# Six pairs of gate projections per layer as seven products of quarters, in a stage of their own

## The chip, the cores and the metric

The kernel runs on one core of one Trainium2 chip. The metric is the device time of one execution in microseconds (us). Before the change the median of three runs is 2574.22 us (2568.73 to 2576.42).

TensorE (PE in the profile) multiplies, ScalarE (ACT), VectorE (DVE) and GpSimd (POOL) do the elementwise work, and SyncE (SP) issues all of this kernel's DMAs from one in-order queue. Each engine carries out its own instructions in the order in which they stand in the built program and waits on semaphores for what the others deliver.

## The reference

Two layers of a decoder trunk over 1024 tokens behind 16 learned meta tokens (L = 1040 columns), width 1024. In each layer one wide projection of the normed input feeds three attention branches and their gates:

```python
h = rmsnorm(x, norm_g)
proj = h @ w_in
(a_q, a_k, a_v, a_f, a_z, b_cq, b_ckv, b_kr, b_z,
 c_q, c_k, c_v, c_z, gates) = jnp.split(proj, np.cumsum(SPLIT_SIZES)[:-1], axis=-1)
y_a = causal_block_attention(..., log_cum)                   # A: 8 heads, forget bias
y_b = causal_block_attention(q_b, k_b, v_b, ...)             # B: latent, 8 heads
y_c = sliding_window_sink_attention(qc, kc, vc, sinks)       # C: banded, window 128
branches = jnp.stack([y_a * silu(a_z), y_b * silu(b_z), y_c * silu(c_z)], axis=2)
proj_br = jnp.einsum('blnw,nwd->blnd', branches, w_branch)
g = jax.nn.sigmoid(gates.reshape(B, L, N_BRANCH, D_MODEL))
return x + jnp.sum(g * proj_br, axis=2) @ w_out
```

`gates` is a product of the 1040 normed tokens (1024 in the second layer, where meta tokens are no longer needed as queries) with 3072 columns of `w_in`: 24 tiles of 128 output channels per layer. Only these are changed.

## The kernel before, in words

Activations lie transposed, channels on the 128 partitions and tokens along the free dimension. Every float32 value that enters a large product is split in two rounded parts, a high and a low one (`split`: ACT writes the high part, DVE or POOL subtracts it from the source for the low part), and `mm3` makes each product of three matmuls: high by high, low activations by high weights, high activations by low weights. The normed input is `hh` and `hl`, eight tiles of 128 channels by 1040 tokens each.

A projection tile (`proj`) is 8 x 3 matmuls for each chunk of tokens: chunks of 264, 264 and 512 columns in the first layer (`FULL`), 512 and 512 in the second (`TOK`). `weights` loads one 512 KB weight tile (`wr`, two buffers), casts it on ACT to `wh` and subtracts on POOL for `wl`.

The stages of a layer, in program order: values of branch A and C (`values`), banded projections (`wq`: rotary keys and queries of branch C; the small rows of the forget gate run beside them in `side_work`), low-rank projections (`lr`, `vb`, `mq`), then forgetting attention (tiles `ks`, `qq`, `ql`), banded attention (`kc`, `cqq`, `cql`, `sP`), latent attention (`kt`, `qt`), the merge of the branches and the output projection. The merge reads the gates back from DRAM (`gate_d`) and applies the sigmoid as a tanh.

The 24 gate tiles, and twelve gate tiles of another kind (`z`, for the SiLU), need nothing but `hh` and `hl`. Before, all 24 are made by `gate`, at places given by two tables. `EARLY` puts two (first layer) or one (second) into the low-rank stage. `PLAN` has one list for each attention stage; each call of `fill` takes the next entry and writes one projection for each letter (`g` a gate, `z` a SiLU gate, `r` and `s` parts of the merge). So these projections fill TensorE while softmax work is under way.

What is written this way is not the final order. The tile framework schedules all instructions of the program against its own timeline when the kernel is built, so matmuls of a gate end up between matmuls of attention, and instructions move over tens of microseconds. The built order is fixed from then on.

Banded attention works in steps of 128 queries for four heads: eight matmuls of 256 columns (`qk`: high and low queries by keys), a reduction on DVE for each head, exponentials on ACT, eight transposes, a split by ACT and DVE, and four matmuls of 512 columns. There are sixteen steps in a layer, eight for each of the two key heads, and one short step for the meta tokens in the first layer. Its loads reuse memory of the forgetting attention and stand behind `rt_d` in SP's queue, which carries the reciprocal row sums (`rcp`) of the last heads there.

## Time and profile before

| | before |
|---|---|
| median of three runs | 2574.22 us |
| profiled execution | 2569.85 us, its span 2567.8 us |
| TensorE busy | 2517.1 us, 98% of the span, 15446 matmuls |
| VectorE, ScalarE, GpSimd busy | 1273.4, 1205.8, 1012.9 us (50%, 47%, 39%) |
| granted TensorE clock, mean | 0.998 |
| DMA queue, share of 16 engines | 38.0% |

A matmul's row shows its whole way through the array, so rows overlap: 350 ns is the mean of a 512-column matmul whose successor starts some 232 ns later. Time per matmul is therefore read from start to start, and a wait shows somewhat too short as idle time.

The stages of the profiled execution, by the rows of the timeline: first layer values to about 85 us, banded projections to 150, low-rank stages to 300, forgetting attention to 645, banded attention to 815, latent attention to 1085, merge and output projection to 1290. The second layer's forgetting attention ends at 1920, its banded attention at 2080, its latent attention at 2360.

### The profile page before, as it was taken

The numbers are of one execution on the slowest core, as the hardware profiler recorded it, in microseconds if no ns is written. First come the engines' busy times: TensorE is split into PE (matmuls) and PEld (weight loads), VectorE is DVE, ScalarE is ACT, GpSimd is POOL, SyncE is SP. The second block draws the span as 40 slices with busy tenths as digits, with TensorE's granted clock in tenths as the row PEclk, the third lists the DMA queues.
The fourth block names the chain that finished last, engine by engine and source line by source line (L and its number), as shares of the span: only waits on it lengthen the run. The fifth ranks groups of instructions, "written<-read, shape, count | busy, mean of one in ns | idle before, by whom it ended". The sixth has DMA issues, their size and how long they took to land.

```text
span 2567.8 us, 42092 instructions
## 1 busy us (share of the span) xinstructions
PE 2517.1 (98%) x15446; PEld 2247.5 (88%) x15446; DVE 1273.4 (50%) x3279; ACT 1205.8 (47%) x2704; POOL 1012.9 (39%) x990
## 2 busy tenths in 40 slices
PE   8999999999999999999999999999999999999998
PEld 7999899999888999899998888888887888887797
DVE  6454355544363445657156463545434623565643
ACT  5234355545374556654233343555435634566433
POOL 2241545443332424463523325454423342353644
PEclk9999999999999999999999999999999999999999
DMA  5244512222634434364333353221326362453532
GB/s 170 62 136 150 189 54 82 73 78 77 172 105 115 129 101 126 102 228 166 114 90 99 97 198 138 66 88 56 98 69 176 100 169 81 124 146 115 183 130 74
DMA packets 137630, 303.39 MB, mean 118 GB/s; under 512 B 22560, under 2 KB 63296, under 8 KB 137424
## 3 DMA queue, kind: packets, MB, share of 16 engines
q1 hardware_dynamic: 137424, 300.71, 38.0%
q8 instruction: 122, 2.00, 0.3%
q14 instruction: 84, 0.69, 0.1%
HBM read 211.98 MB, written 88.66 MB: 117 GB/s over the span
## 4 chain that ended last, share of the span: by engine, by line
PE 79%; DMA 5%; DVE 2%; ACT 2%; POOL 2%; issue 1%; SPq 0%; POOLq 0%; ACTq 0%; DVEq 0%
PE ps_pj L175 14%; PE ps_pj L176 14%; PE ps_pj L177 14%; PE ps_t L268 5%; PE ps_s L1001 3%; PE ps_o L312 3%; PE ps_o L310 2%; PE ps_s L177 2%; PE ps_s L176 2%; PE ps_s L175 2%; PE ps_s L804 1%; PE ps_s L802 1%; PE ps_o L176 1%; PE ps_o L177 1%; PE ps_o L175 1%
## 5 line engine op out<-in xcount | busy, mean ns | idle before, releaser
L158 POOL TENSOR_TENSOR wl<-wr,wh 128x1024 fp32r<-128x1024 f32 (+1 forms) x156 | 376.1, 2411 | 776.7 <-ACT wh L157 653.5
L175 PE MATMUL ps_pj<-hh,wh 128*128 128x512 f32 (+1 forms) x1920 | 672.7, 350 | 3.5 <-ACT gt L657 2.0
L176 PE MATMUL ps_pj<-hl,wh 128*128 128x512 f32 (+1 forms) x1920 | 671.0, 349 | 0.0
L177 PE MATMUL ps_pj<-hh,wl 128*128 128x512 f32 (+1 forms) x1920 | 669.6, 349 | 0.9 <-POOL wl L158 0.9
L175 PEld LDWEIGHTS ps_pj<-hh,wh 128*128 128x128 f32 x1920 | 361.3, 188 | 46.7 <-ACT gt L657 2.6
L177 PEld LDWEIGHTS ps_pj<-hh,wl 128*128 128x128 f32 x1920 | 361.5, 188 | 42.3 <-POOL wl L158 1.1
L176 PEld LDWEIGHTS ps_pj<-hl,wh 128*128 128x128 f32 x1920 | 361.4, 188 | 39.4 <-issue 0.5
L158 DVE TENSOR_TENSOR ptl<-ps_t,pth 128x512 fp32r<-128x512 f32 (+1 forms) x386 | 244.5, 640 | 143.6 <-ACT pth L157 137.8
L260 ACT ACTIVATE P<-P,mn 128x656 f32<-128x656 f32 (+8 forms) x272 | 207.0, 761 | 165.1 <-DVE mn L255 160.5
L157 ACT CAST pth<-ps_t 128x512 fp32r<-128x512 f32 (+1 forms) x386 | 205.7, 546 | 165.3 <-PE ps_t L268 131.9
L157 ACT CAST wh<-wr 128x1024 fp32r<-128x1024 f32 (+1 forms) x156 | 162.1, 1039 | 237.0 <-PE ps_pj L176 134.5
L268 PE MATMUL ps_t<-ident,P 128*128 128x128 f32 x1152 | 186.2, 275 | 0.8 <-DVE ptl L158 0.7
L310 PE MATMUL ps_o<-pth,vp 128*128 128x256 f32 (+1 forms) x640 | 167.2, 277 | 2.7 <-DVE u L281 1.7
L312 PE MATMUL ps_o<-ptl,vp 128*128 128x256 f32 (+1 forms) x640 | 159.4, 287 | 2.7 <-DVE ptl L158 2.5
L298 POOL COPY pmeta<-P 128x16 f32<-128x16 f32 x256 | 49.3, 196 | 270.1 <-ACT P L260 261.9
L1001 PE MATMUL ps_s<-kt,qt 96*128 96x328 f32 (+9 forms) x696 | 146.4, 327 | 2.7 <-DVE mn L255 2.6
L268 PEld LDWEIGHTS ps_t<-ident,P 128*128 128x128 f32 x1152 | 134.2, 140 | 8.6 <-DVE ptl L158 1.5
L310 PEld LDWEIGHTS ps_o<-pth,vp 128*128 128x128 f32 x640 | 120.6, 189 | 11.2 <-ACT pth L157 1.7
L809 POOL TENSOR_TENSOR cm<-ckb,tri 128x128 f32<-128x128 f32 (+1 forms) x136 | 60.3, 445 | 175.2 <-DVE mn L255 171.4
L312 PEld LDWEIGHTS ps_o<-ptl,vp 128*128 128x128 f32 x640 | 120.6, 188 | 9.6 <-DVE ptl L158 5.6
L281 DVE TENSOR_TENSOR u<-ps_o,hv 64x256 f32<-64x256 f32 x128 | 53.9, 421 | 135.4 <-ACT hv L280 120.2
L1001 PEld LDWEIGHTS ps_s<-kt,qt 96*128 96x128 f32 (+1 forms) x696 | 108.0, 186 | 10.1 <-DVE mn L255 5.2
(354 smaller groups left out, 5641.7 us busy)
## 6 DMA issues: line engine op xcount, KB each, us to landing
wr<-in_w_dram SPq DMA_DIRECT2D x108, 512.0 KB
gate_d<-gt SPq DMA_DIRECT2D x72, 256.0 KB
gt<-gate_d SPq DMA_DIRECT2D x24, 520.0 KB
wr<-in_wbr_dram SPq DMA_DIRECT2D x24, 512.0 KB
gt<-gate_d SPq DMA_DIRECT2D x24, 512.0 KB
kn_d<-sg SPq DMA_DIRECT2D x16, 520.0 KB
ckb<-ck_d SPq DMA_DIRECT2D x16, 520.0 KB
kt<-kn_d SPq DMA_DIRECT2D x16, 520.0 KB
```

The source lines that it names most:

```text
L157: nc.scalar.copy(hi, src)
L158: (eng or nc.vector).tensor_tensor(lo, src, _f(hi), ALU.subtract)
L175: nc.tensor.matmul(dst, w1, rh[:, k, c0:c1], start=(k == 0), stop=False)
L176: nc.tensor.matmul(dst, w1, rl[:, k, c0:c1], start=False, stop=False)
L177: nc.tensor.matmul(dst, wl[:, k * P:k * P + m], rh[:, k, c0:c1], start=False, stop=(k == nk - 1))
L260: nc.scalar.activation(s[:rows, :n], s[:rows, :n], AF.Exp, bias=prev, scale=-1.0, accum_out=total)
L268: nc.tensor.transpose(t[:kk, c:c + rows], src, ident[:rows, :rows])
L281: nc.vector.tensor_tensor(u[mine, :n], o[mine, :n], t[mine, :n], ALU.add)
L310: nc.tensor.matmul(dst, vp[:, j + x, vs], ph[:, cols], start=(j + x == 0), stop=False)
L312: nc.tensor.matmul(dst, vp[:, j + x, vs], pl[:, cols], start=False, stop=(diag and x == 1))
L809: nc.gpsimd.tensor_tensor(cm[:rows, :rows], ckb[:rows, d:n], tri[:rows, :rows], ALU.add)
L1001: nc.tensor.matmul(dst, q[:, qi, q0:q0 + rows], kt[:, ki, c0:c1], start=(x == 0), stop=(x == 2))
```

## The change

In each layer the first twelve gate tiles of the list are taken two at a time (`SEVEN = (6, 6)`). A pair is a product of a weight matrix of 256 output channels by 1024 inputs with `h`, 1024 inputs by 1040 (1024) tokens. Both are cut in quarters, halves of the channels and of the inputs by halves of the tokens (`KH = 4` channel tiles, `HW` = 520 or 512 tokens). Eight quarter products become seven, with sums of quarters formed before and after (Strassen's scheme in Winograd's form).

```diff
+        def hidden_sums():
+            for k in range(KH):
+                d = difference(k, (0, 1), (0, 0))        # 3 tensor_tensor on DVE
+                done(0, k, d)                            # split: ACT cast, DVE subtract
+                for i, b_ in ((1, (1, 1)), (3, (1, 0))):
+                    n = tt_.tile([P, HW[0]], F32, tag="tt2", name="tt", bufs=2)[:, :hw]
+                    tensor(n, _f(hidden(0, *b_)[:, k]), d, sub)
+                    tensor(n, n, _f(hidden(1, *b_)[:, k]), add)
+                    done(i, k, n)
+                    d = n
+                yield
+                done(2, k, difference(k, (1, 1), (0, 1)))
+                yield
...
-        values(va, 0, ws, KD, hh, hl, rest, span=1 if first else 2)
+        values(va, 0, ws, KD, hh, hl, rest, between=sums_at, span=1 if first else 2)
...
+        def gate_pairs(n):
+            gs = tc.alloc_tile_pool(name=f"gs{l}", bufs=2, side=B if first else A, reuse_waits="tile")
+            chunks = [(0, hw // 2), (hw // 2, hw)] if first else [(0, hw)]
...
+                split(a1h, a1l, raws[0], eng=nc.gpsimd)
...
+                for f, x, y, op in ((f1, r21, r22, ALU.add), (f2, f1, r11, ALU.subtract),
+                                    (f3, r11, r21, ALU.subtract), (f4, r12, f2, ALU.subtract)):
+                    nc.gpsimd.tensor_tensor(f, x, y, op)
+                for j in (1, 0, 2, 3):
+                    split(s[j][0], s[j][1], fs[j], eng=nc.gpsimd)
+                split(*a22, r22, eng=nc.gpsimd)
...
+                product(a11, b11, (x1, None))
+                product(s[1], t2, (x2, x1))
+                product(a12, b21, (x4, x1))
+                store(0, 0, x4)
+                product(s[0], t1, (x1, x2))
+                product(s[2], t3, (x3, x1), (x2, x2))
+                store(1, 1, x3)
+                product(s[3], b22, (x1, x1))
+                store(0, 1, x1)
+                product(a22, t4, (x2, x2))
+                store(1, 0, x2)
+        gate_pairs(SEVEN[l])
```

Each `product` is 4 x 3 matmuls for a chunk, of 260 columns (two chunks, first layer) or 512 (second); its result leaves PSUM by an ACT copy or by DVE additions. `gate_pairs` stands between the banded projections and the low-rank stage, and both layers have one. The hidden sums (`ths`, eight tiles) are written into the values stage from its fifth (third) block on. The other edits make room: the small rows of `side_work` share tiles, the pairs of rotated rows in the banded projections have two buffers instead of three, `krt` and `ths` have pools of their own, and `vw` is released earlier.

The tables lose the twelve gates. In all there were 9, 7 and 6 gates in the three lists of the first layer and 9, 9 and 5 in the second (forgetting, banded, latent); now there are 3, 4, 3 and 4, 4, 3. The list of the second layer's banded stage shows it:

```diff
-     "gg zg z g . gg zz g gg".split(),
+     "g zg z . . g zz . g".split(),
```

The first place to look at is where the second layer's banded attention begins, on PE: `rcp` is the transpose of the last row sums of the forgetting stage, `pmeta` and `pm,vm` finish its meta keys, `hh,wh`, `hl,wh` and `hh,wl` are projections of the filler, and `kc,cqq` is banded attention. Before:

```order
L312 MATMUL ps_o<-ptl,vp 128x128
L331 MATMUL ps_t<-ident,rcp 16x128
L364 MATMUL ps_t<-ident,pmeta 32x128 x4
L176 MATMUL ps_pj<-hl,wh 128x512
L177 MATMUL ps_pj<-hh,wl 128x512
L175 MATMUL ps_pj<-hh,wh 128x512
```

After:

```order
L336 MATMUL ps_t<-ident,rcp 16x128
L315 MATMUL ps_o<-pth,vp 128x256
L317 MATMUL ps_o<-ptl,vp 128x256
L315 MATMUL ps_o<-pth,vp 128x128
L317 MATMUL ps_o<-ptl,vp 128x128
L369 MATMUL ps_t<-ident,pmeta 32x128 x8
L376 MATMUL ps_o<-pm,vm 128x512 x2
L988 MATMUL ps_s<-kc,cqq 128x256
L990 MATMUL ps_s<-kc,cql 128x256
```

Before, 57 filler matmuls stand between `rcp` and the first `kc,cqq`, and more between the next seven; now there is none, and the whole first step of banded attention (eight such matmuls) and the first two transposes of its exponentials come before the next filler. In the first layer it is the same: 87 filler matmuls of 512 or 264 columns stood between `rcp` and the first `kc,cqq`, and 39 more between that and the eighth; now none.

SP's queue at this place after the change, 16 DMAs in nine rows; the loads of banded attention stand behind `rt_d`, which waits for `rcp`:

```order
L106 DMA rt_d<-rt 8x128 x2
L106 DMA sw<-in_swm_dram 128x512
L106 DMA rb<-rt_d 64x1024 x2
L106 DMA vcr<-vc_d 128x1024
L106 DMA vcr<-vc_d 16x128
L106 DMA kc<-sk_d 128x16
L106 DMA kc<-sk_d 128x1024
L106 DMA cqq<-sq_d 64x1024 x2
L106 DMA cql<-sq_d 64x1024
```

This order is the one of before; in the first layer four stores of gates (`gate_d<-gt`) that stood among the loads are gone. Three more groups of `cqq`, `cql` follow for the other heads.

The third place is the middle of the second layer's banded attention on PE, where the steps of the first key head end (`rcp`) and those of the second begin. Before:

```order
L892 MATMUL ps_o<-pth,vc 128x512
L331 MATMUL ps_t<-ident,rcp 32x128
L867 MATMUL ps_s<-kc,cqq 128x256
L869 MATMUL ps_s<-kc,cql 128x256
L177 MATMUL ps_pj<-hh,wl 128x512
L867 MATMUL ps_s<-kc,cqq 128x256
L869 MATMUL ps_s<-kc,cql 128x256
```

After:

```order
L1015 MATMUL ps_o<-ptl,vc 128x512
L336 MATMUL ps_t<-ident,rcp 32x128
L1013 MATMUL ps_o<-pth,vc 128x512
L988 MATMUL ps_s<-kc,cqq 128x256
L990 MATMUL ps_s<-kc,cql 128x256
L988 MATMUL ps_s<-kc,cqq 128x256
L990 MATMUL ps_s<-kc,cql 128x256
L273 MATMUL ps_t<-ident,sP 128x128 x4
```

The filler matmuls between the steps are gone here: from the sixth step to the fifteenth no filler stands in PE's queue (80 `kc` matmuls, 72 transposes and 31 matmuls of 512 columns in one piece), and then a whole gate tile stands in one block of 48. In the first layer such a piece has 45 `kc` matmuls, 36 transposes and 14 products with `vc`, which is about half as long. In latent attention the pieces without filler that hold over 4.2 us of matmuls add up to 142 us by the durations in the profile before, against 78 us; in forgetting attention to 46 us against 6.

## The prediction

> **What bounds the kernel now.** I read the page first, then the pace of TensorE from the timeline, then the places where it waits.

> ```profile
> span 2567.8 us, 42092 instructions
> PE 2517.1 (98%) x15446; PEld 2247.5 (88%) x15446; DVE 1273.4 (50%) x3279; ACT 1205.8 (47%) x2704; POOL 1012.9 (39%) x990
> PE   8999999999999999999999999999999999999998
> PEclk9999999999999999999999999999999999999999
> ```

> TensorE is the bound nearly everywhere, at full clock, while the others work half the time. So a matmul less is time gained, but only while something keeps TensorE's queue fed. Rows of matmuls overlap, so the price of one is read from start to start, here in second and first layer:

> ```profile
> 1921.16 0.39 PE L177 MATMUL ps_pj<-hh,wl 128*128 128x512 f32 x1
> ...
> 1925.11 0.40 PE L176 MATMUL ps_pj<-hl,wh 128*128 128x512 f32 x1
> ```

> ```profile
> 646.40 0.29 PE L175 MATMUL ps_pj<-hh,wh 128*128 128x264 f32 x1
> ...
> 649.19 0.28 PE L177 MATMUL ps_pj<-hh,wl 128*128 128x264 f32 x1
> ```

> The first pair is 17 matmuls apart, so 3.95 / 17 = 0.232 us for 512 columns; the second 23, so 2.79 / 23 = 0.121 us for 264. By the line through both, 260 columns take 0.1195.

> **Removed: an eighth of the products.** In the first layer a pair took 96 x 0.121 + 48 x 0.232 = 22.8 us and will take 7 x 12 x 2 = 168 x 0.1195 = 20.1; in the second 96 x 0.232 = 22.3 becomes 84 x 0.232 = 19.5. Over six pairs each that is 6 x (2.7 + 2.8) = 33 us. [...]

> **Added, and hidden.** The sums of hidden quarters are 4 x 14 = 56 DVE operations and 16 ACT casts per layer. DVE's nearest row with two SBUF operands takes 0.69 us, so some 39 us per layer, in the values stage:

> ```profile
> L958 DVE TENSOR_TENSOR acc<-acc,gt x80: 420/691/4335, 1116.9 to 2463.8; 128x512 f32<-128x512 f32 x48, 128x264 f32<-128x264 f32 x32
> ```

> ```profile
> 60.00:80.00 20.00, 20.00 (x130) 19.65 (x129) 1.56 (x4) 1.54 (x8) 0.00 (x0) 1.00 0.14 42
> 80.00:100.00 20.00, 20.00 (x134) 18.77 (x133) 2.85 (x7) 2.84 (x13) 0.00 (x0) 1.00 0.12 36
> 1340.00:1360.00 20.00, 20.00 (x130) 19.82 (x129) 2.29 (x6) 1.88 (x11) 0.00 (x0) 1.00 0.14 42
> ```

> In these windows (PE, PEld, DVE, ACT, POOL busy) DVE is idle for 35.6 of 40 us, so the sums cost 0; what spills into the banded projections could cost up to 3. Without that cover the 39 us would delay the rotations there.

> In the new stage POOL makes per pair one difference of 1024 columns and nine operations of 512:

> ```profile
> L158 POOL TENSOR_TENSOR wl<-wr,wh 128x1024 fp32r<-128x1024 f32 (+1 forms) x156 | 376.1, 2411 | 776.7 <-ACT wh L157 653.5
> ```

> ```profile
> 133.32 1.30 POOL L158 TENSOR_TENSOR wvl<-wr,wvh 128x512 fp32r<-128x512 f32 x1 [0.72 <-ACT wvh L157]
> ```

> 2.4 + 9 x 1.3 = 14.1 us against 20 of TensorE: hidden, with 6 us left for loading the next weights. At the entry it is not: in the built order POOL starts the sums behind the last rotation of the banded projections, and the first product with a sum needs four operations (5.2 us) on top of the rotation's POOL and DVE work (about 4). In the first layer TensorE has 48 matmuls (5.7 us) for this, so 4 us wait; in the second another product stands ahead and 1 us is left. Together +5, between 0 and 10. The stores of the results and weight loads share SP's queue; nobody behind them is short. The pools with two buffers instead of three wait for stores while TensorE has four chunks in PSUM: 0.

> **Moved: cover taken from attention.** Twelve gates per layer, some 137 us of ready work, leave the queue between attention's matmuls. The largest effect is at the entry of banded attention. In the second layer:

> ```profile
> 1920.38 0.27 PE L331 MATMUL ps_t<-ident,rcp 128*16 128x128 f32 x1
> ...
> 1935.07 0.28 PE L867 MATMUL ps_s<-kc,cqq 128*128 128x256 f32 x1
> 1937.71 0.36 PE L867 MATMUL ps_s<-kc,cqq 128*128 128x256 f32 x1 [0.39 <-DMA cqq<-sq_d]
> 1941.06 0.35 PE L867 MATMUL ps_s<-kc,cqq 128*128 128x256 f32 x1 [0.39 <-DMA cqq<-sq_d]
> ...
> 1944.96 0.28 PE L869 MATMUL ps_s<-kc,cql 128*128 128x256 f32 x1
> ```

> ```profile
> 1921.26 0.62 SPq L101 DMA_DIRECT2D rt_d<-rt  x2
> ...
> 1936.43 0.44 SPq L101 DMA_DIRECT2D cql<-sq_d  x1
> ```

> ```profile
> 1924.00:1927.00 3.00, 3.00 (x17) 2.39 (x16) 0.41 (x1) 1.16 (x2) 2.89 (x5) 1.00 1.01 229
> 1942.00:1945.00 3.00, 2.78 (x13) 1.97 (x13) 0.00 (x0) 0.00 (x0) 0.00 (x0) 1.00 1.04 328
> ```

> The loads stand behind `rt_d`, which waits for `rcp`, and with a DMA share of 1.0 they last until the fourth head's matmul runs at 1944.96, 24.6 us after `rcp`. Fillers cover that now, up to some 3 us. In the built order after the change they are gone: PE has four `vp` matmuls, eight transposes, two `pm` matmuls (1.9 us) and the step itself (1), and then must wait about 21. Net +18: at least +14, if the loads run at the best rate of these windows; at most +21 with the first transposes' wait for the exponentials. Everything behind it on PE is held. The first layer:

> ```profile
> 644.65 0.27 PE L331 MATMUL ps_t<-ident,rcp 128*18 128x128 f32 x1
> ...
> 668.57 0.18 PE L869 MATMUL ps_s<-kc,cql 128*16 128x16 f32 x1 [0.24 <-DMA cql<-sq_d]
> ```

> 23.9 us, less 3.5 for four gate stores (0.8 MB at some 230 GB/s) that are no longer among the loads, less 2.5 of own matmuls, less 3 that is waited there already: +14, between 10 and 18.

> A wait of that length also costs clock:

> ```profile
> 12.96 0.64 PE L454 MATMUL ps_pj<-wvh,hh 128*128 128x320 f32 x1 [3.21 <-ACT hh L157]
> ```

> ```profile
> 10.00:15.00 5.00, 1.95 (x6) 1.52 (x7) 3.10 (x11) 4.78 (x13) 5.00 (x4) 0.79 1.09 342
> 15.00:20.00 5.00, 5.00 (x34) 5.00 (x34) 2.88 (x11) 3.07 (x13) 5.00 (x4) 0.87 1.06 379
> ```

> After 3.2 us of idle TensorE two windows show a clock of 0.79 and 0.87, 5 x (0.21 + 0.13) = 1.7 us lost. Two waits: +3, between 2 and 6.

> Next, the steps of banded attention without filler:

> ```profile
> L873 DVE CUSTOM_DVE_ANT_0 sP<-ps_s,sw,nsink 128x256 f32<-128x256 f32 x64 | 28.3, 477 | 23.3 <-PE ps_s L869 23.3
> L158 DVE TENSOR_TENSOR ptl<-ps_t,pth 128x512 fp32r<-128x512 f32 x32 | 21.6, 683 | 0.6 <-ACT pth L157 0.2
> L902 DVE TENSOR_TENSOR u<-ps_o,stt 64x128 f32<-64x128 f32 x64 | 15.6, 283 | 24.8 <-ACT stt L900 23.3 <-DMA y_d<-u 1.1
> ```

> These are sixteen steps, so (28.3 + 21.6 + 15.6) / 16 = 4.1 us of DVE per step, while PE's share is 8 x 0.12 + 8 x 0.11 + 4 x 0.232 = 2.8. With a filler DVE is hidden; without, a step takes at least 4.1. DVE is not busy all the time even where little fills, as the latent stage shows:

> ```profile
> 900.00:920.00 20.00, 20.00 (x140) 18.72 (x138) 8.94 (x25) 9.31 (x21) 2.97 (x4) 1.00 0.29 81
> 1020.00:1040.00 20.00, 19.30 (x140) 17.83 (x140) 16.12 (x50) 16.19 (x41) 15.16 (x23) 1.00 0.70 183
> 1040.00:1060.00 20.00, 18.50 (x135) 16.88 (x134) 15.87 (x45) 15.66 (x38) 17.83 (x23) 1.00 0.20 75
> 2240.00:2260.00 20.00, 18.13 (x129) 15.79 (x128) 15.81 (x47) 16.55 (x39) 16.60 (x18) 1.00 0.77 200
> ```

> There it is busy for 0.8 of the time, so a step would take 5.1. I take 4.6, the middle. The second layer's piece without filler is about nine steps by its 80 `kc` matmuls, 72 transposes and 31 products: 9 x 4.6 = 41 us against 25 of PE, less about 1 that DVE still works off behind the next block of 48: +15, between 10 and 21. The first layer's, four and a half steps: 20.7 less 12.3 less 1: +7, between 3 and 10.

> Latent attention without filler: the covered window 900:920 shows no idle time, the three bare ones 0.7 to 1.9 of 20, and the gaps behind modelled ends hide about as much again. So 0.05 to 0.25 us per us of such PE work, 0.15 in the middle; the pieces grow from 78 to 142 us: +10, between 3 and 16. Forgetting attention's pieces are short (5 to 9 us) and DVE lags little: +2, between 0 and 8.

> **The sum**: -33 + 5 + 18 + 14 + 3 + 15 + 7 + 10 + 2 = +41 us on the profiled execution's 2569.85. That execution lies 4.4 below the median of the runs; +41 on the median 2574.22 is 2615.

> **Rivals.**
> 1. Cover survives: faster. The place is the entry of banded attention. If TensorE found its loads landed, both waits and their clock (35) would go; if steps also ran at PE's 2.8 us (22 more), -33 + 5 + 12 = -16 remains, 2558. It decides once the loads take under some 10 us after `rcp`. For it: two entries only, and loads could be better packed. Against: the share of 1.0 says that the data itself takes that time. Chance 0.07.
> 2. The entries wait, but the bare steps run near PE's pace, since work lags and is made up in the next block: 22 less, and half of latent attention's 10: 2588. For it: single steps without filler are short. Against: nine in a row. Chance 0.18.
> 3. The clock falls in the bare pieces too. Scattered idle time there is 7 to 9% in the windows above, at a clock of 1.00, which speaks against it; if steps of 2.8 us PE in 4.6 drop it to half, the 37 us of banded pieces and parts of the next blocks lose about 20 us: 2635. [...] Chance 0.10.
> 4. The change does not make its product cheaper: POOL's 14.1 us and a weight load in series exceed 20 us per pair, TensorE waits for sums. At 23 us a pair 12 x 3 = 36 more: 2651. The 6 us of slack speak against it. Chance 0.07.

> **How the numbers follow.** The forecast has 0.58, and 2599 to 2633 if each term goes half way to its lower or its upper end. The range 2583 to 2645 leaves out rival 1 and most of rival 4. A measurement tells about 0.3% (8 us) from no change: below 2566 is faster, above 2582 slower. Faster is rival 1; the same is its weak form and the low edge of rival 2, 0.08; slower the rest, 0.85.

> **What would show it.** Right: the paired gates take 20 us a pair on PE, from start to start; two waits of PE of 15 to 21 us on `cqq` or `cql` right behind `rcp` of the forgetting stage, with a dip of the clock behind them; idle PE in the second half of banded attention with DVE near 0.9; no wait on POOL's sums inside the gate stage but for its entry. Wrong: waits for `cqq` under 8 us, or idle time of PE under 80 us in the whole span, against 51 now.

## Result, and the profile after

The changed kernel takes 2715.95 us (median of four runs, 2713.64 to 2725.55), the kernel before 2575.11 beside it on the same chip. The ratio is 1.056, 95% interval 1.053 to 1.059: 141 us slower. The forecast was slower, but by 41 us, and the range ended at 2645. The profiled execution has a span of 2713.5 us, 145.7 more than before.

The page of the changed kernel, first the span, then busy time, then TensorE's share and its granted clock in 40 slices:

```profile
span 2713.5 us, 42693 instructions
PE 2548.7 (94%) x15518; PEld 2264.2 (83%) x15518; DVE 1400.5 (52%) x3517; ACT 1225.5 (45%) x2742; POOL 1119.2 (41%) x1086
PE   8989999999979999999979998999999789999998
PEclk9989999999989999999979999999999899999999
```

Before, both rows of tenths were nines but for the first and the last slice. Now TensorE shows holes in slices spread over the whole program, and the clock has holes beside them. What TensorE waits for (engine, tile, line, releaser: us in total, times, longest):

```profile
PE ps_s L988 <- DMA cqq<-sq_d: 26.0, 9, 9.3
PE ps_o L180 <- ACT s L162: 13.9, 2, 9.8
PE ps_s L459 <- ACT wvh L162: 13.3, 1, 13.3
PE ps_s L923 <- DVE mn L260: 7.1, 11, 1.6
...
PE ps_pj L180 <- ACT wh L162: 6.7, 2, 5.8
PE ps_s L180 <- ACT wh L162: 6.5, 1, 6.5
PE ps_t L180 <- ACT wh L162: 6.2, 2, 4.2
...
PE ps_o L180 <- DVE ro L235: 4.4, 1, 4.4
```

The first row is the entry of banded attention. It was forecast, but as one wait of 15 to 21 us in each layer; the longest in each is this one:

```profile
773.16 0.17 PE L988 MATMUL ps_s<-kc,cqq 128*16 128x16 f32 x1 [7.18 <-DMA cqq<-sq_d]
...
2128.96 0.55 PE L988 MATMUL ps_s<-kc,cqq 128*128 128x256 f32 x1 [9.30 <-DMA cqq<-sq_d]
```

The second row is the entry of the new stage (9.8 us in the first layer, 4.1 in the second). `wvh`, the largest single wait, is the second layer's values stage, to which the prediction had given nothing. The rows on `wh` are the end of the new stage (5.8 and 6.5 us before the next weights are there), the second layer's values stage (4.2) and the banded projections (2.1); `ro` are the rotations in the banded projections.

The pairs themselves do what they should. From the start of one pair to the start of another, in the first layer from the second pair to the sixth, in the second layer from the fourth to the sixth:

```profile
191.53 0.28 PE L180 MATMUL ps_pj<-hh,wh 128*128 128x260 f32 x1
...
272.06 0.28 PE L180 MATMUL ps_pj<-hh,wh 128*128 128x260 f32 x1
```

```profile
1582.83 0.39 PE L180 MATMUL ps_pj<-hh,wh 128*128 128x512 f32 x1
...
1621.79 0.39 PE L180 MATMUL ps_o<-hh,wh 128*128 128x512 f32 x1
```

That is 80.53 us for four pairs, 20.1 each, and 38.96 for two, 19.5 each, as forecast.

To place the loss I take, for each matmul, the distance to the start of the next one beyond what its columns need at the pace of the prediction (0.232 us for 512, and not under 0.109, the median distance from a transpose of 128 columns to the next matmul in the profile before). The sum of these excesses is 74.6 us before and 253.6 after, 179 more, against 33 of work less. The experiments say where the 179 lie.

### The profile page after: what moved, and what is told of

Read it like the earlier page. It is cut to its first block, busy times and chain, and to the rows that moved or that the text cites. A ratio compares the mean times of both kernels' runs of the same rounds, so it can differ in the third digit from the quotient of the medians.

```text
span 2713.5 us, 42693 instructions
## 1 busy us (share of the span) xinstructions
PE 2548.7 (94%) x15518; PEld 2264.2 (83%) x15518; DVE 1400.5 (52%) x3517; ACT 1225.5 (45%) x2742; POOL 1119.2 (41%) x1086
## 4 chain that ended last, share of the span: by engine, by line
PE 78%; DVE 9%; DMA 5%; ACT 3%; issue 3%; POOL 1%; SPq 1%; POOLq 0%; DVEq 0%; ACTq 0%
PE ps_pj L180 12%; PE ps_pj L181 12%; PE ps_pj L182 12%; PE ps_t L273 5%; PE ps_s L1122 3%; PE ps_s L180 3%; PE ps_s L182 3%; PE ps_s L181 3%; PE ps_o L317 3%; PE ps_o L315 2%; PE ps_o L180 2%; PE ps_o L181 2%; PE ps_o L182 2%; PE ps_t L181 2%; PE ps_t L182 2%
## 5 line engine op out<-in xcount | busy, mean ns | idle before, releaser
L163 POOL TENSOR_TENSOR wl<-wr,wh 128x1024 fp32r<-128x1024 f32 (+2 forms) x156 | 361.0, 2315 | 708.8 <-ACT wh L162 672.0
L180 PE MATMUL ps_pj<-hh,wh 128*128 128x264 f32 (+2 forms) x1476 | 517.4, 351 | 10.7 <-ACT wh L162 6.7
L181 PE MATMUL ps_pj<-hl,wh 128*128 128x264 f32 (+2 forms) x1476 | 515.9, 350 | 0.0
L182 PE MATMUL ps_pj<-hh,wl 128*128 128x264 f32 (+2 forms) x1476 | 513.0, 348 | 0.5 <-POOL wl L163 0.5
L180 PEld LDWEIGHTS ps_pj<-hh,wh 128*128 128x128 f32 x1476 | 280.6, 190 | 45.7 <-ACT wh L162 7.7
L182 PEld LDWEIGHTS ps_pj<-hh,wl 128*128 128x128 f32 x1476 | 280.2, 190 | 32.4 <-POOL wl L163 1.2
L181 PEld LDWEIGHTS ps_pj<-hl,wh 128*128 128x128 f32 x1476 | 280.6, 190 | 30.8 <-issue 0.5
L162 ACT CAST wh<-wr 128x1024 fp32r<-128x1024 f32 (+2 forms) x156 | 156.8, 1005 | 251.7 <-PE ps_pj L181 130.6
L317 PE MATMUL ps_o<-ptl,vp 128*128 128x256 f32 (+1 forms) x640 | 165.5, 295 | 6.1 <-DVE ptl L163 5.0
L317 PEld LDWEIGHTS ps_o<-ptl,vp 128*128 128x128 f32 x640 | 122.4, 191 | 17.4 <-DVE ptl L163 14.2
L315 PEld LDWEIGHTS ps_o<-pth,vp 128*128 128x128 f32 x640 | 122.9, 192 | 16.5 <-ACT pth L162 7.5
L260 DVE CUSTOM_DVE_ANT_0 P<-ps_s,ckb 128x16 f32<-128x16 f32 (+7 forms) x128 | 56.7, 443 | 95.3 <-PE ps_s L925 63.6
```

Source lines behind the costliest of these rows:

```text
L162: nc.scalar.copy(hi, src)
L163: (eng or nc.vector).tensor_tensor(lo, src, _f(hi), ALU.subtract)
L180: nc.tensor.matmul(dst, w1, rh[:, k, c0:c1], start=(k == 0), stop=False)
L181: nc.tensor.matmul(dst, w1, rl[:, k, c0:c1], start=False, stop=False)
L182: nc.tensor.matmul(dst, wl[:, k * P:k * P + m], rh[:, k, c0:c1], start=False, stop=(k == nk - 1))
L260: nc.vector.tensor_tensor_reduce(s[:rows, x0:x1], t[:rows, x0 - c0:x1 - c0], b[:, x0 - s0:x1 - s0], 1.0, prev, ALU.add, ALU.min, mn[:rows, ...
```

## Experiments

Differences below are medians against the kernel before in the same comparison; the changed kernel stands 140.8 us above it.

**1. Only the moved cover.** The kernel before, with the changed kernel's lists `PLAN` and the twelve gates ahead of time:

```diff
...
+        for _ in range(12):
+            gate(gs)
...
```

> The kernel before with the shorter lists of fillers of the changed one, and the twelve gates of each layer as ordinary projections in one stage behind the banded projections: no products of quarters, no sums, no tiles for them. All work is there, only moved. Theory A (moved cover: the extra time lies where attention lost its fillers; read from the traces by stage, attention pays 105 us more than before): about 2680 us, 105 over the kernel before. Rival B (the stage of quarters itself costs nearly all beyond the prediction's 69 us for moved cover): about 2645. Rival C (all of the extra time is cover: 141 + 33): about 2749.

Measured 2674.44 us, ratio 1.039 (1.037 to 1.040), 100 us above the kernel before: theory A. So moving twelve ordinary gates per layer to a stage of their own costs 100 us, where the prediction's terms for it add up to 69 with the clock. By place (excess of this run less that of the kernel before, 105.9 in the profiled executions):

| place | predicted | measured |
|---|---|---|
| entry of banded attention, first / second layer | 14 / 18 (and 3 of clock) | 13.3 / 17.4 |
| steps of banded attention, first / second layer | 7 / 15 | 13.5 / 14.2 |
| latent attention, both | 10 | 15.3 |
| forgetting attention ahead of that entry, first / second layer | 2 for both | 16.5 / 10.9 |
| all else | 0 | 4.8 |

The row of the entries also holds 3.2 and 2.9 us that are lost at half clock (0.50 from 755.10 to 775.60 in the first layer) and not in waits. So the waits cost about 10 and 14.5 us, less than the 14 and 18 forecast, and the clock 6 where 3 was forecast; that the sum comes out right is in part luck. Where an entry ends and the steps begin is a choice, which moves about 1 us between the first two rows.

The forecast failed most in forgetting attention. Its loss does not lie all over the stage, but in a few pieces. Two of them by windows (us, then busy time of PE, PEld, DVE, ACT, POOL, granted clock, DMA share and GB/s), a long one and a short one:

```profile
550.40:561.10 10.70, 8.43 (x55) 6.36 (x53) 10.37 (x39) 8.63 (x24) 5.17 (x10) 0.97 0.22 59
647.30:649.50 2.20, 2.20 (x22) 2.20 (x21) 1.29 (x3) 1.93 (x6) 2.20 (x4) 1.00 0.07 28
```

The first has 6.8 us of TensorE work and no filler, and lost 3.9 us; DVE is busy for 10.37 of 10.70 us. The second has 2.2 us of work and loses nothing; DVE works 1.3. In both layers no piece without filler of up to some 2.5 us of work lost more than some 0.1 us, and every longer one lost time: those of 3.0, 4.7, 6.5, 6.8 and 8.2 us lost 0.7, 2.3, 2.3, 3.9 and 5.1 in the first layer, those of 3.3, 4.6, 6.6 and 9.4 lost 2.1, 0.9, 4.7 and 2.8 in the second. In the other long pieces DVE is busy for only 0.55 to 0.87 of the time, so there its work alone does not set the time; how the steps on DVE and ACT share in it was not taken apart.

**2. Without sums of hidden quarters, and with their tiles alone.** One run reads plain quarters and has neither sums nor tiles, the other keeps the tiles `ths` set aside:

```diff
...
-        sums_ = hidden_sums()
+        sums_ = iter(())
...
-            t1, t2, t3, t4 = ((t[0][:, :, :hw], t[1][:, :, :hw]) for t in ths)
+            t1, t2, t3, t4 = ((hidden(0, *b_), hidden(1, *b_)) for b_ in ((0, 0), (0, 1), (1, 0), (1, 1)))
...
```

> The changed kernel without the sums of hidden quarters and without the tiles for them; the products read quarters of the hidden values instead, as many and as long, and the sums of weights stay. Left out are 56 DVE sums and 16 splits per layer and 66 KB per partition. The prediction had them at 0: then 2716, within 5. Theory D (their memory delays others: in the second layer the value weights come to lie where the output stage still reads, and TensorE waits 13.3 us on wvh; in the first layer the weights of the next stage lie where the last product still reads; and the sums delay the banded rotations): 25 to 28 us of waits and half clock go in the second layer's values stage, 5 to 15 elsewhere, about 2680.

> The run without sums of hidden quarters (2671, 45 below the changed kernel), but with the eight tiles for them set aside as in the changed kernel; they are never written or read. Left out are the same sums. Theory D1 (the memory alone delays the second layer's value weights, and the first layer's weights behind the stage): the 28 us of the second layer's values stage come back, and some 5 us in the first layer: about 2703. Theory D2 (the sums' work on DVE and ACT, which blocks what is queued behind it, delays): about 2671 as without tiles.

Without both 2671.08 us (ratio 1.037, 1.036 to 1.039), 44 less than the changed kernel; with the tiles alone 2694.16 (1.047, 1.045 to 1.048), 19 less. So the memory set aside costs 25 us, and making and reading the sums 19 more; D1 and D2 each hold in part. The memory shows in the second layer's values stage. Four kernels over that stage: before, changed, without both, tiles alone.

```profile
1295.30:1364.30 69.00, 69.00 (x449) 67.31 (x448) 29.26 (x62) 20.65 (x60) 13.21 (x8) 1.00 0.30 88
```

```profile
1365.70:1463.50 97.80, 78.01 (x448) 72.35 (x446) 71.80 (x118) 30.31 (x76) 14.73 (x8) 0.86 0.21 62
```

```profile
1351.10:1420.20 69.10, 69.10 (x448) 67.41 (x447) 29.28 (x62) 20.66 (x60) 13.20 (x8) 1.00 0.29 88
```

```profile
1348.90:1436.60 87.70, 74.33 (x431) 69.02 (x430) 29.26 (x62) 21.20 (x60) 12.64 (x8) 0.88 0.23 69
```

The same 448 matmuls take 69 us, 98, 69 and 88 (some records are missing in the last), and the clock falls with the wait (1.00, 0.86, 1.00, 0.88). The reason stands on ACT, in the changed kernel (first) and in the one without tiles:

```profile
1391.47 0.58 ACT L162 CAST hh<-ps_o 128x512 fp32r<-128x512 f32 x1 [1.87 <-DVE ps_o L217]
1391.96 1.49 ACT L162 CAST wvh<-wr 128x720 fp32r<-128x720 f32 x2
```

```profile
L162 ACT CAST wvh<-wr x4: 787/795/820, 1351.3 to 1359.7; 128x720 fp32r<-128x720 f32 x4
```

The casts of the value weights start right behind the last `hh`, the end of the norm that reads the output stage's `xn`, 26 us into the stage; without the tiles they start 0.2 us into it, while that norm still goes on. In the second layer the pools `kt1` and `th1` are set aside on the right side ahead of `va1`, so `va1` moves on to memory where `xn` still is: by the addresses in the built programs `wvh` overlaps `xn` in the changed kernel and with the tiles alone, and lies clear of it without them. The rest of the 25 us lies behind this stage, part of it at the second layer's entry of the new stage, where TensorE waits 4.2 us with the tiles alone and not at all without them.

The sums lengthen this wait. DVE makes some of them (L564 to L575) between the steps of the norm (L217), and TensorE waits 13.3 us for `wvh` where it waits 9.8 with the tiles alone:

```profile
1389.50 0.68 DVE L565 TENSOR_TENSOR tt<-hl 128x512 f32<-128x512 f32 x1
1390.10 0.68 DVE L575 TENSOR_TENSOR tt<-tt,hl 128x512 f32<-128x512 f32 x1
1390.70 0.74 DVE L217 SCALAR_TENSOR_TENSOR ps_o<-xn,gcol,ps_t 128x512 f32<-128x512 f32 x1
```

The excess of this stage is 29 us with the sums and 21 without, of which about 5 come back in the stages behind it. More of the 19 us lies in the first layer: from the end of the values stage to forgetting attention the excess is 36.0 us in the changed kernel and 25.0 with the tiles alone. Some 8 of these 11 us lie where the new stage ends:

```profile
286.63 1.14 ACT L162 CAST wvh<-wr 128x512 fp32r<-128x512 f32 x2 [11.13 <-PE ps_t L182]
...
298.11 0.59 PE L180 MATMUL ps_pj<-hh,wh 128*128 128x264 f32 x1 [5.75 <-ACT wh L162]
```

By the addresses in the built program the value weights `wvh` of the low-rank stage lie where the tiles `t` of the sums are, so their casts wait for the last products that read `t`. Until then they hold the buffers `wr`, and the loads of the next weights start at 293.27, behind the last stores in SP's queue. With the tiles alone, which no product reads, these casts run at 266.00 and 271.10, the loads start at 270.02, and TensorE does not wait there. Some 6 us more lie in the first layer's latent attention, where the built order is another one; they were not taken apart.

**3. Without sums of weights.** The products read plain quarters of the weights instead, as many and as long, and the tiles of the sums are not there:

```diff
...
-                for j in (1, 0, 2, 3):
-                    split(s[j][0], s[j][1], fs[j], eng=nc.gpsimd)
+                split(a2h, a2l, raws[1], eng=nc.gpsimd)
...
+                s = (a21, a22, a21, a12)
```

> The changed kernel without the sums of quarters of weights: the products use plain quarters of the two gates' weights, as many and as long; POOL makes two ordinary differences per pair, and the eight tiles of sums are not there. The prediction's term for them was +5 (a wait at the entry): then 2711. Theory E (both entries, 9.8 and 4.1 us, and the second layer's leaving, 6.5 us, hang on these sums and their tiles, with half a clock behind each): about 2690. If POOL bounded the stage inside, more than that: each pair would get shorter than 19.5 us.

2687.00 us (1.044, 1.042 to 1.045), 28 less than the changed kernel: theory E. In the second layer, from the end of values to forgetting attention, changed and without sums:

```profile
1463.50:1806.80 343.30, 329.07 (x1548) 270.90 (x1547) 135.35 (x206) 108.06 (x189) 162.44 (x112) 0.98 0.40 131
```

```profile
1452.10:1779.70 327.60, 324.97 (x1549) 267.74 (x1548) 135.04 (x206) 97.06 (x165) 109.38 (x64) 1.00 0.42 137
```

One matmul record apart there are as many, 15.7 us less, and 2.6 us idle instead of 14.2. The second layer's wait at the end of the stage goes with these sums; the first layer's stays (6.4 us), and belongs to the hidden sums of experiment 2. At the entry the sums do not just take their time on POOL, they start late. In the first layer of the changed kernel POOL first waits for stores:

```profile
169.06 1.26 POOL L741 TENSOR_TENSOR sf<-wr 128x512 f32<-128x512 f32 x1 [3.31 <-DMA sq_d<-sg]
173.17 1.26 POOL L741 TENSOR_TENSOR sf<-wr 128x512 f32<-128x512 f32 x1 [2.85 <-DMA sq_d<-sg]
```

The tiles of these sums lie, by the addresses in the built program, on the rotated rows `sg` of the banded projections, which SP is still storing. Inside the stage TensorE does not wait on POOL: 117.16 of 117.20 us are busy from 175.1 to 292.3 in the changed kernel.

**4. The stage with all cover kept.** All 24 gates stay as fillers, so twelve are computed twice.

```diff
...
-                i = todo.pop(0)
+                i = twice.pop(0)
...
```

> The stage of quarters as in the changed kernel, with its memory and sums, but all 24 gates of a layer also stay as ordinary fillers with the longer lists of the kernel before: twelve per layer are computed twice. TensorE has 12 x 19.8 = 237 us more work than the kernel before. By the prediction's price of the stage (+5) 2575 + 237 + 5 = 2817. By theory F (the stage costs what the traces show outside of attention, 74 us, mostly in the second layer's values stage and around the pairs) 2575 + 237 + 74 = 2886. If the waits outside of attention were caused by the missing fillers after all, it is the former.

2885.35 us (1.121, 1.119 to 1.123), 311 above the kernel before. Six pairs at the measured 20.1 us and six at 19.5 are 238, so the stage costs 73: theory F. Attention behind it is back at the excess of the kernel before (latent attention of the first layer has 3 us more). The pieces add up: 100 (cover) + 73 (stage) - 33 (products) = 140, and 141 were measured; 44 + 28 = 72 is the stage taken apart. That the last two agree so well is in part luck, since the second layer's wait at the entry goes in either of the two runs.

**5. A gate on each side of the pairs.**

```diff
...
+        gate(fl)
         gate_pairs(SEVEN[l])
...
+        gate(fl)
...
```

> The changed kernel, with one ordinary gate ahead of the pairs of quarters and one behind them in each layer; they are taken from the latent projections (two in the first layer, one in the second) and from forgetting attention (one in the second). If the waits of 9.8 and 4.1 us at the entries and of 5.8 and 6.5 us at the ends, with the half clock behind each (9 us in all), only lack ready work of some 11 us, up to 35 us go there, and where the four gates are missing now 5 to 15 come back: about 2692. Rival (the weights behind the stage wait for memory that the last product still reads, so a gate in between moves the wait and the gates' old places pay): about 2716.

2684.56 us (1.043, 1.041 to 1.044), 29 less than the changed kernel. The waits at both ends of the stage are gone: the second layer's row of experiment 3 now reads

```profile
1442.80:1782.80 340.00, 336.78 (x1597) 277.30 (x1596) 137.01 (x206) 110.85 (x192) 165.50 (x113) 1.00 0.40 136
```

with 3.2 us idle at full clock. Three of the four gates come from the low-rank stages (`EARLY`), one from the second layer's list. In the first layer POOL shows no wait for stores at the entry any more. So this stage lacked only some 11 us of ready work, and the four gates were missed little where they came from.

**6. Gates to the entry of banded attention.**

```diff
...
-     "g zzg . . . g zz . g".split(),
+     "ggg zz . . . . zz . g".split(),
...
```

> The changed kernel; in the list of fillers of banded attention two gates of each layer move from its later steps to its start. By the prediction's terms the entries' waits (15.4 and 15.9 us idle in the run with ordinary gates, 17.0 and 19.6 us with what follows from them) then find 24 us of work: 25 to 31 us less, and the steps that lose a gate pay 8 to 16 more; about 2700. Rival (a gate covers as much at any place, or TensorE reaches the entry earlier and waits as long): 2716, within 5.

2719.48 us (1.058, 1.055 to 1.060): no gain. In the first layer:

```profile
757.42 0.29 PE L182 MATMUL ps_pj<-hh,wl 128*128 128x264 f32 x1
...
764.00 0.40 PE L182 MATMUL ps_pj<-hh,wl 128*128 128x512 f32 x1
...
790.36 0.17 PE L988 MATMUL ps_s<-kc,cqq 128*16 128x16 f32 x1 [7.25 <-DMA cqq<-sq_d]
```

```profile
L336 PE MATMUL ps_t<-ident,rcp x1: 270/270/270, 777.5 to 777.5; 128*18 128x128 f32 x1
```

Filler runs here 13 to 20 us ahead of `rcp`, which starts the loads; behind it nothing ready is left, and the wait is the 7.2 us of before. A gate that is ready goes ahead of what makes the queue wait, so a place in the list does not keep it for the wait.

**7. Extra matmuls in that wait**, tied to it by reading `kc`:

```diff
...
+                if kv == 0:
+                    for _ in range(2):
+                        t = psum("pj")
+                        for k in range(12):
+                            nc.tensor.matmul(t, kc[:, 0:P], kc[:, P:P + 512],
...
```

> The run with ordinary gates in a stage (2674), with 24 extra matmuls of 512 columns (5.6 us at full clock) on banded keys ahead of the first scores, where TensorE waits 7.8 and 9.5 us for queries at a half clock that lasts 20.5 and 17.1 us. Their results are not used. If the wait costs its idle time alone, the time stays at 2674 or rises by 1 to 2 (where the extra work outlasts the wait). If the half clock behind it costs as the records say (9.4 - 6.0 and 7.8 - 4.6 us beyond idle time), the half clock ends with the extra work, and 4 to 6 us go: about 2669.

2670.15 us (1.038, 1.036 to 1.039) against 2674.44 (1.037 to 1.040) without them; the intervals overlap. In the trace the built order also moved a gate behind the entry, and the excess of forgetting and banded attention with the 11.2 us of extra work counted as loss is 98.5 us against 98.3. So by these two runs this work in the wait cost nothing that shows, and whether the full clock behind it (1.00 from 755.25 to 772.30, against 0.50 from 755.10 to 775.60 without these matmuls) gains anything stays open: behind the first wait the next heads' loads are still to come.

**8. Short bare pieces; the first layer alone; two pairs.** All three build on experiment 5. The lists of the first layer, as an example:

```diff
...
-    ("g z . z . . . g . . z . z . g . .".split(),
-     "g zzg . . . g zz . g".split(),
-     "g g . z . z g . . . zzr s . . sss s s".split()),
+    ("g . . z z . . . . . gz . z . g . g".split(),
+     "g zzg g . g g zzg . .".split(),
+     ". . . z . z . . . . zzr s . . sss s s".split()),
...
```

> The flanked kernel (2685) with as many gates, in other places: all six of latent attention go to forgetting and banded attention, and the lists there are chosen by the built order so that pieces of TensorE work without filler stay short. In the run with ordinary gates, pieces up to 4.1 us of work cost nothing and each us beyond it 0.6 us. In forgetting and banded attention the built order of the flanked kernel has pieces that by this rule cost 13.7 + 8.5 + 14.8 + 12.8 = 50 us, and this one 5.6 + 0.4 + 12.4 + 0 = 18. Theory (the length of bare pieces sets the price, and latent attention, whose steps lag little, pays 0.1 to 0.15 us per us of the 70 us that it loses): 50 - 18 - 9 = 23 less, about 2662. Rival (each gate covers the same 2.5 to 3.5 us wherever it stands, as moving twelve of them cost 100 us in all): 2685, within 5.

> The first layer as in the kernel with short bare pieces, the second as in the kernel before (24 ordinary gates as fillers, no tiles of sums). If layers add up: the second layer of the flanked kernel shows 109 us between and beyond its matmuls where the kernel before shows 25; 84 less 15 that short pieces already save, less the 17 that its cheaper products save, so 52 below the kernel with short bare pieces: about 2610 if that gives 2662, still 37 above the kernel before. Rival (the second layer's losses come from the first's new order, or its memory): it stays within 20 of the kernel with short bare pieces.

> Two pairs of quarters instead of six, in the first layer alone, flanked by one ordinary gate on each side; 18 gates stay as fillers, the second layer is as in the kernel before. The products save 2 x 2.7 = 5.5 us. Theory (the stage has a fixed price, whatever its length: 13 us around it in the first layer of the flanked kernel, most of it from the sums of hidden quarters): 2573 + 13 - 5.5 + 0 to 10 for the six gates of cover = 2580 to 2590. Rival (the price falls with the number of pairs): 2573 or below.

With short bare pieces 2690.87 us (1.046, 1.045 to 1.048): not 23 less, but 6 more, and neither theory. Why is on TensorE, at the start of latent attention in both layers:

```profile
924.90 0.55 PE L1128 MATMUL ps_s<-kt,qt 96*16 96x16 f32 x4 [14.70 <-DMA qt<-qr_d]
...
2261.19 0.46 PE L1128 MATMUL ps_s<-kt,qt 96*128 96x144 f32 x1 [15.76 <-DMA qt<-qr_d]
```

The six gates that I took from latent attention had covered the loads at its entry; the 30.5 us of new waits ate the gain. This entry had cost 3.3 us in the changed kernel and was in no theory of mine. Without these waits banded attention's excess falls from 46.7 to 20.6 us in both layers together, 26 less, where the rule of 0.6 us said 21. In forgetting attention it said 10 and nothing came (56.7 and 56.4 us): as a rule to plan by it holds for the one and not for the other. Its bound of 4.1 us came from a stretch of experiment 1 (593.60 to 597.60) in which 13 of the matmuls are filler; without it the bound is the 2.5 us given there.

The first layer alone takes 2621.88 us (1.018, 1.017 to 1.020), 69 below that, where 52 were expected, since the second layer's part of the new wait goes too. The second layer's stages are within 1.1 us of their excess before (but 1.6 less in the output). Layers add up. Two pairs take 2592.99 (1.008, 1.006 to 1.009), slower than the kernel before by 20, 3 above the expected band. Around the stage the excess is 11.7 us more than before, near the 13 us that six pairs cost in the first layer of experiment 5: most of the price does not fall with the number of pairs, and it is twice what two pairs save; another 9.5 us lie in the first layer's latent attention, which gave three gates. No version here is as fast as the kernel before.

## Why the prediction was wrong

- **Products, -33:** right. A pair took 20.1 and 19.5 us from start to start, as forecast.
- **"In these windows DVE is idle for 35.6 of 40 us, so the sums cost 0":** failed, 44 us. The idle time is there, but the price is not in DVE's load. The edits that make room were costed at nothing, and the memory of the tiles alone takes 25 us, most of it because the second layer's value weights come to lie where `xn` is still read. The other 19 us have three places: some 11 before forgetting attention in the first layer, mostly because the next value weights lie where the last products still read `t`; some 3 in the second layer, where the sums stand between the steps of a norm; and some 6 in the first layer's latent attention, the cause of which stays open.
- **Entry of the new stage, +5:** failed, 28 us. The wait itself was 9.8 and 4.1 us instead of 4 and 1, because the sums of weights also wait for the memory of rows that are still being stored. The second layer's end of the stage (6.5 us until the next weights are there) was not in the sum at all: the prediction says of SP's queue that "nobody behind them is short".
- **Entries of banded attention, +14 and +18:** right as sums, 13.3 and 17.4, but these hold 6 us of clock, so the waits were some 4 us shorter each than forecast. The loads take their time as forecast: in the first layer of experiment 1 the fourth head's matmul runs 20.4 us after `rcp`, which is the forecast 23.9 - 3.5. But the wait comes as one of 7 to 9 us and several short ones behind it, not as one of 15 to 21. By the prediction's own signs the first layer's wait of 7.2 us is wrong (under 8), and the second layer's of 9.3 lies between.
- **Bare steps of banded attention, +15 and +7:** the second layer right (14.2), the first twice as much (13.5).
- **Latent attention, +10:** 15.3, inside its range.
- **"Forgetting attention's pieces are short (5 to 9 us) and DVE lags little: +2":** failed, 27. The lengths were right, the price was not: only pieces of up to some 2.5 us of work cost nothing, and those of 5 to 9 us lost 0.9 to 5.1 us each.
- **Clock, +3:** failed. In the changed kernel some 40 us of excess beyond idle time lie in half-clock stretches (granted clock 0.50), 2 in the kernel before. They are inside the stages' numbers above, so they are no term of their own.

Of the 100 us missed, two thirds lie in the new stage: 73 against 5. The other third is cover, 100 against 69. Slower was forecast and came, but by a sum in which the largest part of what was missed, the hidden sums and their memory, stood at nothing. Of the rivals, the third came nearest in kind (the clock falls in bare pieces, to 0.84 in the mean from 2180 to 2200 us in the changed kernel's second layer). The fourth is ruled out, since the pairs take what was forecast and get no shorter without the sums of weights (20.16 and 19.55 us). The range was too narrow because every rival but that one was about attention, and none was about the new stage's own edges or its memory.

## What to carry over

Work that fills waits is not worth its length: taking 12 of 24 fillers per layer away cost three times what the cheaper products saved. A new stage is priced at its two edges first: what does the first product need that isn't there, and which weights, memory and queue stand behind the last one. And each set of tiles is asked whom it displaces and on what it lies: a pool ahead of another moves that one onto memory that may still be in use, and three of the new waits (the value weights on `xn` and on `t`, the sums on rows being stored) are of this kind.

## What the hardware showed

The half clock comes far sooner than I had taken from the one wait of 3.21 us in the trace before. In the run of experiment 1, three windows in a row:

```profile
557.05:560.46 3.41, 1.66 (x10) 1.16 (x10) 3.25 (x12) 3.36 (x9) 2.60 (x5) 1.00 0.00 0
560.46:563.87 3.41, 3.41 (x12) 2.83 (x11) 2.39 (x9) 2.60 (x8) 2.50 (x7) 0.51 0.44 156
563.87:567.28 3.41, 3.41 (x18) 2.83 (x17) 0.65 (x1) 0.22 (x1) 0.00 (x0) 0.99 0.00 0
```
